# Moving low parts and half of a norm's sums to GpSimd, taking the norm's roots by columns, and placing loads and casts elsewhere in a two-layer hybrid backbone

## The chip, the core and the metric

The kernel runs on one core of a Trainium2 chip. A core has a matrix engine (TensorE, PE in the profile, with its weight loads as PEld), a vector engine (VectorE, DVE), a scalar engine (ScalarE, ACT), a general engine (GpSimd, POOL), a queue for transfers (SyncE, SP) and 16 DMA engines. Each engine works through its instructions in a fixed order and waits on semaphores. The metric is the device time of one execution in microseconds.

## The reference

`x` (1024 tokens, width 1024) goes through two layers and a final RMS norm. In the words of the reference:

```python
# layer 0 (even): conv branch A and bidirectional RG-LRU branch B
va, vg, ga, xb, gb = split(h @ w_in)
u = depthwise_conv(va * sigmoid(vg), conv_w, conv_b)
y_a = silu(layernorm(u)) * silu(ga)
y_b = rglru(xb) * silu(gb)
x = x + gate * (concat([y_a, y_b]) @ w_out)
# layer 1 (odd): pooling mixer
u, g = split(modulate(rmsnorm(x)) @ w_in)
x = x + gate * ((pool_and_group_matmul(u) * scale * silu(g)) @ w_out)
return rmsnorm(x) * final_g
```

`shift`, `scale` and `gate` of a layer come from a product of `silu(c)` with that layer's modulation matrix. All is float32. The layer norm over the width is `(u - mean) * rsqrt(var + eps)`, with `eps` 1e-5.

## The kernel before

Activations lie with the width on the 128 partitions (8 blocks, `u0` to `u7`) and the tokens along the row, in two halves of 512. A float32 product is made of three products of a shorter type: each operand is split into a high part (a cast, by ScalarE) and a low part (source less high part, by VectorE or GpSimd); TensorE adds high x high, high x low and low x high. Names ending in `h` and `l`, or beginning with `wh` and `wl`, are these parts. For the ga, woa, v, g and wo products a two by two block scheme ("quad": accumulators `qa`, `qb`, `qc`, seven products with operands `b11`, `t1`, ... `t4`) replaces the eight products.

The stages of the program in time: folds of weights (to 83 us), the input products and the LRU (to 510), the ga quads (to 587), `wob` (the half of `w_out` that meets branch B: 8 output blocks of two token halves with 24 matmuls each, 587 to 694), `woa` (the half that meets branch A, four quads, 694 to 780), more weight folds and the second layer's norm (to 828), v and g quads, the output product `wo` in two parts, and the final norm.

Up to the end of `wob` the order on each engine is the order in which the code calls `on()` (line 476 is its issuing line, so nearly all rows of that part read L476): `vec`, `act`, `gp`, `cast` and `sp` append to VectorE, ScalarE, GpSimd, casts of ScalarE and SyncE's queue. From `woa` on (`fixed[0] = False`) a scheduler orders the instructions by their readiness and priorities.

What the prediction touches, in the order before. `block_split` makes the low parts of the ga operands (8 of 128x1024) and `gated_split` those of branch B (`ybl0` to `ybl7`), all on VectorE. `wob_split(m)` casts the weights of output block m and makes their low part `wl_wob` on GpSimd. `ln_mean` multiplies the running sum `lnsum` by ones (`mu`), after three of the eight steps of block 0. `ln_square` subtracts `mu` and squares; `ln_add` sums the eight squares on VectorE, into `lnsum` again. `ln_root` multiplies this by ones (`ms_ln`, 512 wide), takes the root on ScalarE (`sq_ln`, 512 wide); `ln_scale` begins with a reciprocal of 512 columns on VectorE and multiplies the eight blocks. `ln_silus`, `ga_mult`: silu, and the product with silu(ga); `wob_evict` adds a block of `wob`, times the gate, to `xp` (ScalarE and GpSimd up to block 4, VectorE after). The second layer's modulation is a row sum of a 128x512 half of the matrix times `cH` (silu of half of `c`): `mod_half` makes 32 of them, one accumulator column each, 12 in the `wob` stage and 20 between the `woa` quads, with small sums `m` and `a` behind each. `rstd_cols` takes the second layer's root already by columns: four one-column matmuls, a root and reciprocal of 128x4, a diagonal (`dg`, identity times the four columns) and a matmul with ones. `split_x` makes the operands of the v product, `fo` the evictions of folds, and `y_operand` loads, casts and subtracts the operands of `wo` (`yr_b`, `y_b11h`); `b_wo` is a copy of an accumulator by ScalarE.

Of the kernel before, what the change touches and what calls it, by code (L numbers as in the profile page):

```python
# [54 lines left out]
def body(ctx, tc, xT, ctxT, cc, ccol, modT, modW, win, gw, wout, wu, grp, wg, wo1, small, edge, ident, outT):  # L55
# [1114 lines left out]
    def gated_split(n):  # L1170
# [3 lines left out]
        vec(nc.vector.tensor_tensor, out=bl[n], in0=raw, in1=bh[n].bitcast(F32), op=sub)  # L1174
# [121 lines left out]
    def half_c(q):  # L1296
        sp(cH, cc[0, HALF[q]].partition_broadcast(P))
        act(cH, cH, AF.Silu)

# [52 lines left out]

    def ln_scale(h):
        vec(nc.vector.reciprocal, out=lnr[h], in_=lnrt[h])
# [18 lines left out]
    mraws = []  # L1373

    def mod_load(q, n):
        mraws.append(ttile(f"mod1_{n}_{q}"))
        (sp if staged[0] else nc.sync.dma_start)(mraws[-1], modT[1, n, :, HALF[q]])

    def mod_half(q, n):
        raw = mraws.pop(0)  # L1380
        vec(nc.vector.scalar_tensor_tensor, out=raw, in0=raw, scalar=1.0, in1=cH, op0=mult, op1=mult,
            accum_out=m1p[:, n, q : q + 1])

    def mod_halves():
        for n in range(NFIX, 2 * KT):
            mod_load(0, n)
            mod_half(0, n)
            yield
        load_c(0, cH, HALF[1])
        for n in range(2 * KT):  # L1390
            mod_load(1, n)
            mod_half(1, n)
# [701 lines left out]
```

## Time and profile before

| | |
|---|---|
| median of 3 runs | 1328.02 us (1327.42 to 1328.87) |
| profiled execution | 1327.48 us, span 1325.7 us |
| granted TensorE clock, mean | 0.984 |
| busy: PE, DVE, ACT, POOL | 1275.4, 1170.1, 650.8, 393.8 us |
| instructions | 15823 |

The span runs from the first to the last instruction, and the profiled execution's own time is 1.8 us longer. A row of the waits names who waited, for whom, the sum, the count and the longest. A row of the timeline has start, duration, engine, line, operation, tiles written and read, shapes and how many instructions it joins; in brackets the idle time before it and what ended it. Durations of matmuls overlap, since they are pipelined: their pace is read from their starts.

### The profile page before, as it was taken

What the parts mean: (1) busy time and instruction counts of PE and PEld (TensorE: products, weight loads), DVE (VectorE), ACT (ScalarE), POOL (GpSimd) and SP (SyncE); (2) the same over time, 40 slices, a digit from 0 to 9 for tenths busy, and PEclk for the clock granted to TensorE, in tenths of its full rate; (3) what the DMA queues carried; (4) which work ended last, traced back from release to release, by engine and by line L of the source; (5) the groups of instructions that cost most, each with busy time, mean ns of one, the idle gap of its engine ahead of it and who ended that gap; (6) DMA issues with size and microseconds to landing.
All of it is one profiled execution on the core that took longest, in us unless ns stands there. A gap on an engine that the chain in (4) does not pass through costs nothing.

```text
span 1325.7 us, 15823 instructions
## 1 busy us (share of the span) xinstructions
PE 1275.4 (96%) x5552; PEld 1019.6 (77%) x5552; DVE 1170.1 (88%) x1790; ACT 650.8 (49%) x949; POOL 393.8 (30%) x214
## 2 busy tenths in 40 slices
PE   8999999999999999989899989899999999989996
PEld 3468888888888888867687878688878888768784
DVE  7959999999999999998988877998999987877875
ACT  5343666566566633555724345734333334634542
POOL 3063765577656626763410022000000000000002
PEclk9999999999999999999999999899999999999997
DMA  9963111112111284474556476244333334868613
GB/s 360 385 210 142 57 42 62 52 61 72 40 64 41 80 297 175 140 291 165 185 200 225 161 251 191 72 151 151 112 105 126 111 120 134 309 206 274 236 64 127
DMA packets 92083, 206.96 MB, mean 156 GB/s; under 512 B 8803, under 2 KB 28643, under 8 KB 92005
## 3 DMA queue, kind: packets, MB, share of 16 engines
q1 hardware_dynamic: 80100, 193.38, 42.3%
q10 hardware_dynamic: 11904, 12.59, 2.8%
q8 instruction: 43, 0.70, 0.2%
q14 instruction: 36, 0.29, 0.1%
HBM read 149.31 MB, written 56.62 MB: 155 GB/s over the span
## 4 chain that ended last, share of the span: by engine, by line
PE 70%; DVE 13%; DMA 10%; ACT 3%; issue 2%; POOL 1%; SPq 1%; ACTq 0%; POOLq 0%; DVEq 0%
PE gb L476 7%; PE vg L476 7%; PE va L476 7%; PE xb L476 6%; PE fold L282 4%; PE g L476 4%; PE qb_ga L476 2%; PE wob L476 2%; PE qc_ga L476 2%; PE qa_ga L476 2%; PE xbc L476 2%; DMA mod<-modT 1%; DMA wr_wu<-wu 1%; PE qb_v L989 1%; PE qb_v L991 1%
## 5 line engine op out<-in xcount | busy, mean ns | idle before, releaser
L476 DVE SCALAR_TENSOR_TENSOR conv<-u,sm,conv 128x505 f32<-128x505 f32 (+7 forms) x229 | 156.1, 746 | 0.9
L1914 POOL TENSOR_TENSOR o<-x,rr 128x256 f32<-128x256 f32 (+1 forms) x9 | 8.0, 926 | 455.0 <-ACT rr L1902 452.0
L476 POOL TENSOR_TENSOR l<-l,l 128x1280 f32<-128x1280 f32 (+1 forms) x23 | 63.9, 2794 | 83.3 <-DVE l L476 68.2
L476 ACT ACTIVATE l<-g,sm 128x512 f32<-128x512 f32 (+1 forms) x96 | 58.6, 618 | 57.8 <-PE g L476 57.0
L282 PE MATMUL fold<-graw,wu 128*128 128x512 f32 x128 | 58.5, 619 | 1.4 <-DMA wu<-wu 1.4
L104 POOL TENSOR_TENSOR wl_wu<-wr_wu,wh_wu 128x1024 fp32r<-128x1024 f32 x8 | 19.2, 2416 | 121.0 <-DVE gl L104 101.8
L476 PE MATMUL wob<-ybh,wl_wob 128*128 128x512 f32 x128 | 50.9, 397 | 4.4 <-POOL wl_wob L476 4.4
L476 PE MATMUL wob<-ybh,wh_wob 128*128 128x512 f32 x128 | 52.4, 409 | 0.7 <-ACT wh_wob L476 0.7
L282 PEld LDWEIGHTS fold<-graw,wu 128*128 128x128 f32 x128 | 25.2, 199 | 34.1 <-issue 30.3
L476 DVE SCALAR_TENSOR_TENSOR conv<-cL,wsum,conv 128x505 f32<-128x505 f32 (+7 forms) x75 | 51.2, 745 | 0.2
L103 ACT CAST wq_v<-wr_v 128x512 fp32r<-128x512 f32 x48 | 28.2, 620 | 45.6 <-DMA wr_v<-wfold 14.8
L476 PE MATMUL wob<-ybl,wh_wob 128*128 128x512 f32 x128 | 50.6, 395 | 0.0
L476 PE MATMUL gb<-h0l,wh_gb 128*128 128x512 f32 x128 | 49.8, 389 | 0.0
L476 PE MATMUL gb<-h0h,wh_gb 128*128 128x512 f32 x128 | 49.8, 389 | 0.0
L476 PE MATMUL vg<-h0l,wh_vg 128*128 128x512 f32 x128 | 49.8, 389 | 0.0
L476 PE MATMUL vg<-h0h,wl_vg 128*128 128x512 f32 x128 | 49.8, 389 | 0.0
L476 PE MATMUL vg<-h0h,wh_vg 128*128 128x512 f32 x128 | 49.8, 389 | 0.0
L476 PE MATMUL va<-h0h,wh_va 128*128 128x512 f32 x128 | 49.8, 389 | 0.0
L476 PE MATMUL va<-h0l,wh_va 128*128 128x512 f32 x128 | 49.8, 389 | 0.0
L476 PE MATMUL va<-h0h,wl_va 128*128 128x512 f32 x128 | 49.8, 389 | 0.0
L476 PE MATMUL gb<-h0h,wl_gb 128*128 128x512 f32 x128 | 49.8, 389 | 0.0
L476 DVE TENSOR_TENSOR_SCAN l<-l,l 128x256 f32<-128x256 f32 (+1 forms) x32 | 48.7, 1522 | 1.1
(695 smaller groups left out, 4376.4 us busy)
## 6 DMA issues: line engine op xcount, KB each, us to landing
mod<-modT SPq DMA_DIRECT2D x20, 512.0 KB, 8.0
x_part<-xp SPq DMA_DIRECT2D x32, 256.0 KB, 3.7
mod<-modT SPq DMA_DIRECT2D x32, 256.0 KB, 5.0
wr_v<-wfold SPq DMA_DIRECT2D x16, 512.0 KB, 4.2
wr_g<-wg SPq DMA_DIRECT2D x16, 512.0 KB, 4.9
wr_wo<-wo SPq DMA_DIRECT2D x16, 512.0 KB, 3.8
y_b<-y SPq DMA_DIRECT2D x24, 256.0 KB, 3.6
y_t<-y SPq DMA_DIRECT2D x24, 256.0 KB, 2.8
```

The lines of the kernel that those rows point to most:

```text
L103: return (nc.scalar.copy(hi, src), eng.tensor_tensor(out=lo, in0=src, in1=hi.bitcast(F32), op=sub))
L104: eng.tensor_tensor(out=lo, in0=src, in1=hi.bitcast(F32), op=sub))
L282: nc.tensor.matmul(ps, w[:, kc], gs[i], start=(i == 0), stop=(i == 3))
L476: last[eng] = f(*args, **kw)
L989: nc.tensor.matmul(ps, hi, xh[k], start=(first and k == 0), stop=False, skip_group_check=not first)
L991: nc.tensor.matmul(ps, hi, xl[k], start=False, stop=False, skip_group_check=not first)
L1914: nc.gpsimd.tensor_tensor(out=o[:, k - k0], in0=v, in1=rr, op=mult)
```

## The change

Seven edits. (1) Four of the eight ga low parts (`htl`, r = 1) and `ybl0` to `ybl3` go from VectorE to GpSimd; `wl_wob0` and `wl_wob5` to `wl_wob7` go from GpSimd to VectorE, and the casts of `wob_split` stand before the evictions of their block. (2) The two `mu` matmuls stand after seven of eight steps of block 0. (3) Of a half's squares, those of blocks 2 to 5 are added up on GpSimd into that of block 1, the last two and the join on VectorE. (4) The layer norm's roots are taken by columns, with an identity loaded into the spare end of `lnsum0`. (5) Of the second layer's modulation halves 16 are summed in the `wob` stage and 16 in the first of the `woa` stage, loaded in fours or pairs, and `m`, `a` are made by four wide operations at the end. (6) The second layer's identity is loaded early into the spare end of `n1acc0`; the stores of `x1` are issued one eviction later; the casts of `b11` and `b21` of v have priority. (7) Three operands of the second part of `wo` are loaded where they were loaded and cast before, and cast later.

The norm's place, on GpSimd, at the begin of `wob`. Before (`xp` are the residual blocks, `wo` the evicted ones):

```order
L476 TENSOR_TENSOR wl_wob1_4722<-wr_wob1_4674,wh_wob1_4721 128x1024
L476 TENSOR_TENSOR xp0_0_4701<-xp0_0_4701,wo_0_0_4851 128x512
L476 TENSOR_TENSOR xp0_1_4703<-xp0_1_4703,wo_0_1_4856 128x512
L476 TENSOR_TENSOR wl_wob2_4863<-wr_wob2_4725,wh_wob2_4862 128x1024
L476 TENSOR_TENSOR xp1_0_4854<-xp1_0_4854,wo_1_0_4920 128x512
L476 TENSOR_TENSOR xp1_1_4859<-xp1_1_4859,wo_1_1_4959 128x512
L476 TENSOR_TENSOR wl_wob3_4970<-wr_wob3_4866,wh_wob3_4969 128x1024
```

and now:

```order
L476 TENSOR_TENSOR ybl3_4588<-ybl3_4588,ybh3_4668 128x1024
L476 TENSOR_TENSOR wl_wob1_4724<-wr_wob1_4675,wh_wob1_4723 128x1024
L476 TENSOR_TENSOR lsq1_0_4812<-lsq1_0_4812,lsq2_0_4815 128x512
L476 TENSOR_TENSOR lsq1_0_4812<-lsq1_0_4812,lsq3_0_4818 128x512
L476 TENSOR_TENSOR lsq1_0_4812<-lsq1_0_4812,lsq4_0_4822 128x512
L476 TENSOR_TENSOR lsq1_0_4812<-lsq1_0_4812,lsq5_0_4826 128x512
L476 TENSOR_TENSOR xp0_0_4702<-xp0_0_4702,wo_0_0_4860 128x512
L476 TENSOR_TENSOR xp0_1_4704<-xp0_1_4704,wo_0_1_4865 128x512
L476 TENSOR_TENSOR wl_wob2_4872<-wr_wob2_4727,wh_wob2_4871 128x1024
L476 TENSOR_TENSOR lsq1_1_4855<-lsq1_1_4855,lsq2_1_4858 128x512
```

The additions of squares (`lsq`) have come between the weights' low parts. On ScalarE, where the two roots were taken (`sq_ln`), before:

```order
L476 ACTIVATE wo_1_0_4920<-wob1_0_4894,m0_176 128x512
L476 ACT_TABLE_LOAD
L476 ACTIVATE sq_ln0_4929<-ms_ln0_0_4926,eps_l_139 128x512
L476 ACTIVATE wo_1_1_4959<-wob1_1_4895,m0_176 128x512
L476 CAST wh_wob3_4969<-wr_wob3_4866 128x1024
L476 ACTIVATE wo_2_0_5001<-wob2_0_4975,m0_176 128x512
L476 ACTIVATE sq_ln1_5009<-ms_ln1_5007,eps_l_139 128x512
L476 ACTIVATE wo_2_1_5044<-wob2_1_4976,m0_176 128x512
```

and now the end of the eight silus of half 0 with the root of half 1 (`rc_ln1`):

```order
L476 ACTIVATE u3_1879<-u3_1879,sm_131 128x512
L476 ACTIVATE u7_3237<-u7_3237,sm_131 128x512
L476 ACT_TABLE_LOAD
L476 ACTIVATE rc_ln1_5048<-ms_ln1_5021,eps_l_139 128x4
L476 CAST wh_wob4_5084<-wr_wob4_4973 128x1024
L476 ACTIVATE wo_2_1_5090<-wob2_1_4995,m0_176 128x512
```

The root of half 1 stood before the silus of half 0 and now stands behind them. TensorE's matmul with the diagonal of half 1 stands between the two halves' last products of block 2 and block 3. On VectorE, the end of `woa`, before:

```order
L1535 SCALAR_TENSOR_TENSOR x1_7_6078<-qb_woa6_6081,m0_176,x1_7_6078 128x512
L1525 TENSOR_TENSOR n1acc0_5580<-n1acc0_5580,n1q6_1_0_6190 128x512
L535 SCALAR_TENSOR_TENSOR mod1_11_1_6193,m1p_3670<-mod1_11_1_6193,cH_3671 128x512
L535 SCALAR_TENSOR_TENSOR mod1_12_1_6198,m1p_3670<-mod1_12_1_6198,cH_3671 128x512
L535 SCALAR_TENSOR_TENSOR m1_178<-m1p_3670,sm_131 128x1
L535 SCALAR_TENSOR_TENSOR mod1_13_1_6203,m1p_3670<-mod1_13_1_6203,cH_3671 128x512
```

and now:

```order
L1562 SCALAR_TENSOR_TENSOR x1_7_6084<-qb_woa6_6087,m0_176,x1_7_6084 128x512
L104 TENSOR_TENSOR gl_3_0_6272<-graw_3_0_6269,gh_3_0_6271 128x1024
L1552 TENSOR_TENSOR n1acc0_5603<-n1acc0_5603,n1q6_1_0_6196 128x512
L104 TENSOR_TENSOR gl_3_1_6278<-graw_3_1_6275,gh_3_1_6277 128x1024
L203 RECIPROCAL rc_n10_6212<-rc_n10_6212 128x4
L205 TENSOR_TENSOR dg_n10_6219<-n1acc0_5603,rc_n10_6212 128x512
```

The halves (`mod1`) and small sums are no longer between the last eviction and the diagonal `dg_n10`.

The diff, cut to its core:

```diff
@@ before: line 1070
         htl.append([d2tile(f"htl{i}_{r}", F32R) for r in range(2)])
-        for r in range(2):
-            vec(nc.vector.tensor_tensor, out=htl[i][r], in0=hraw[i][r], in1=hth[i][r].bitcast(F32), op=sub)
+        for r, by in enumerate((vadd, gp)):
+            by(out=htl[i][r], in0=hraw[i][r], in1=hth[i][r].bitcast(F32), op=sub)
@@ before: line 1171
         cast(bh[n], raw)
-        vec(nc.vector.tensor_tensor, out=bl[n], in0=raw, in1=bh[n].bitcast(F32), op=sub)
+        (gp if n < KH else vadd)(out=bl[n], in0=raw, in1=bh[n].bitcast(F32), op=sub)
@@ before: line 1261
-    def wob_split(m):
+    def wob_split(m, by=None):
         if m < KT:
-            gws[KT + m] = raw_split(obs.pop(m), f"wob{m}")
+            gws[KT + m] = raw_split(obs.pop(m), f"wob{m}", by)
@@ before: line 1277
         fill(3 if n < 4 else 1)
+        if n == 2:
+            sp(idln, ident)
         if n == 3:
-            wob_split(0)
+            wob_split(0, vadd)
         if n == 4:
                 xp_load(0, h)
+            sp(cH, cc[0, HALF[0]].partition_broadcast(P))
         if n == 5:
@@ before: line 1293
-    def half_c(q):
-        sp(cH, cc[0, HALF[q]].partition_broadcast(P))
-        act(cH, cH, AF.Silu)
-
+    idln = lnacc[0][:, H : H + P]
     lnmu, lnsq = {}, {}
@@ before: line 1338
     def ln_add(j, h):
-        if j > 0:
-            vec(nc.vector.tensor_tensor, out=lnacc[h][:, :H] if j == KT - 1 else lnsq[h],
-                in0=lnsq[h], in1=lsq.pop((j, h)), op=add)
-
-    lnrt, lnr = {}, {}
+        if 1 < j < 6:
+            gp(out=lsq[1, h], in0=lsq[1, h], in1=lsq.pop((j, h)), op=add)
+        elif j > 5:
+            vadd(out=lnsq[h], in0=lnsq[h], in1=lsq.pop((j, h)), op=add)
+        if j == KT - 1:
+            vadd(out=lnacc[h][:, :H], in0=lnsq[h], in1=lsq.pop((1, h)), op=add)
+    def ln_squares(h, js):
+        for j in js:
+            ln_square(j, h)
+            if j > 1:
+                ln_add(j - 1, h)
+        if j == KT - 1:
+            ln_add(j, h)
+    lnsum, lnrt, lnr = {}, {}, {}
+    def ln_cols(h):
+        lnsum[h], lnr[h] = banks(f"ms_ln{h}", h)
+        for c in range(H // P):
+            on("pe", nc.tensor.matmul, lnsum[h][:, c : c + 1], lnacc[h][:, c * P : (c + 1) * P], ones[:, 0:1],
+               start=True, stop=True)
+    def ln_diag(h):
+        r = hpool.tile([P, H // P], F32, tag="rc", name=f"rc_ln{h}")
+        act(r, lnsum[h][:, : H // P], AF.Sqrt, bias=eps_l)
+        vec(nc.vector.reciprocal, out=r, in_=r)
+        lnrt[h] = ttile(f"dg_ln{h}")
+        vec(nc.vector.tensor_tensor, out=lnrt[h].rearrange("p (c t) -> p c t", t=P),
+            in0=idln.unsqueeze(1).to_broadcast([P, H // P, P]),
+            in1=r.unsqueeze(2).to_broadcast([P, H // P, P]), op=mult)
     def ln_root(h):
-        ps, lnr[h] = banks(f"ms_ln{h}", h)
-        on("pe", nc.tensor.matmul, ps, ones, lnacc[h][:, :H], start=True, stop=True)
-        lnrt[h] = ttile(f"sq_ln{h}")
-        act(lnrt[h], ps, AF.Sqrt, bias=eps_l)
+        on("pe", nc.tensor.matmul, lnr[h], ones, lnrt[h], start=True, stop=True)
     def ln_scale(h):
-        vec(nc.vector.reciprocal, out=lnr[h], in_=lnrt[h])
         for j in range(KT):
@@ before: line 1370
-    mraws = []
-
...
+    mraws, halved = [], [0, 0]
+    def mod_load(*raws):
+        for raw in raws:
+            q, n = divmod(halved[0], 2 * KT)
+            (sp if staged[0] else nc.sync.dma_start)(raw, modT[1, n, :, HALF[q]])
+            mraws.append(raw)
+            halved[0] += 1
     def mod_halves():
...
+        for raw in mraws:
+            q, n = divmod(halved[1], 2 * KT)
+            vec(nc.vector.scalar_tensor_tensor, out=raw, in0=raw, scalar=1.0, in1=cH, op0=mult, op1=mult,
+                accum_out=m1p[:, n, q : q + 1])
+            halved[1] += 1
+        mraws.clear()
+    def mod_pairs():
+        n = halved[0]
+        for t in [d2tile(f"mod1_{n}_{i}") for i in range(2)]:
+            mod_load(*[t[:, h] for h in HALF])
+    def mod_four(alloc):
+        mod_load(*[alloc(f"mod1_{halved[0]}_{i}") for i in range(4)])
@@ before: line 1422
                     next(steps[h])
-                if k == 2:
-                    for h in range(2):
-                        ln_mean(h)
+            for h in range(2):
+                ln_mean(h)
         for h in range(2):
             if m == 0:
...
+                if h == 0:
+                    act(cH, cH, AF.Silu)
+                    ln_squares(0, range(KT))
+                    mod_pairs()
+                else:
+                    ln_squares(1, range(3))
+                    for q in range(2):
+                        wob_evict(0, q)
+                    wob_split(2)
+                    wob_load(3)
+                    ln_squares(1, range(3, KT))
+            elif h == 0:
+                if m == 2:
+                    ln_root(0)
+                    ln_cols(1)
+                wob_evict(m, 0)
+                if m == 2:
+                    ln_scale(0)
+                    for part in range(2):
+                        ln_silus(0, part)
+                    ln_diag(1)
+                    mod_pairs()
+                elif m == 3:
+                    ln_silus(1, 0)
+                    mod_halves()
+                    for i in range(KH):
+                        ga_mult(i, 0)
+                        ga_mult(KH + i, 0)
+                elif m == 4:
+                    w0 = wquad_load([wout[q, 0] for q in range(2)], "woa0")
+                elif m > 5:
+                    mod_halves()
+                if 4 < m < 7:
+                    mod_four(ttile)
             else:
-                wob_evict(m, h)
+                if m == 1:
+                    ln_cols(0)
+                elif m == 2:
+                    ln_root(1)
+                if m < 4:
+                    wob_split(m + 2, vadd if m == 3 else None)
+                    wob_load(m + 3)
+                wob_evict(m, 1)
+                if m == 1:
+                    ln_diag(0)
+                    mod_halves()
+                elif m == 2:
+                    ln_scale(1)
+                elif m == 3:
+                    ln_silus(1, 1)
+                    for i in range(KH):
+                        ga_mult(i, 1)
+                        ga_mult(KH + i, 1)
+                if m > 3:
+                    wob_split(m + 2, vadd)
+                    wob_load(m + 3)
             if m < 2:
                     ga_load(4 * m + 2 * h + q)
-            if m >= 4:
-                mod_steps(2)
-            if (m, h) == (4, 0):
-                w0 = wquad_load([wout[q, 0] for q in range(2)], "woa0")
-        if m > 0:
-            wob_split(m + 2)
-            wob_load(m + 3)
-    mod_steps(0)
+    sp(cH, cc[0, HALF[1]].partition_broadcast(P))
+    act(cH, cH, AF.Silu)
     xouts.pop()()
@@ before: line 1515
     nacc = [atile("n1acc0"), atile("n1acc1")]
+    idn = nacc[0][:, H : H + P]
+    nc.sync.dma_start(idn, ident)
...
     fold2 = fold(2, wr_tile, vtile, d2tile, [None, None, dtile, dtile])
     for m in range(0, KT, 2):
+        mod_four(vtile)
         w0 = woa(m, w0, (lambda: wo_weights(m + 2)) if m < KT - 2 else None)
...
+        mod_halves()
+    mm1 = m1[:, 0, : 2 * KT]
+    nc.vector.tensor_tensor(out=mm1, in0=m1p[:, :, 0], in1=m1p[:, :, 1], op=add)
+    nc.vector.tensor_tensor(out=mm1, in0=mm1, in1=col(O_MB + 3 * KT, 2 * KT), op=add)
+    nc.vector.scalar_tensor_tensor(out=a1[:, 0], in0=m1[:, 0, KT : 2 * KT], scalar=1.0, in1=col(O_NG + KT, KT),
+                                   op0=add, op1=mult)
     idD = cH[:, :P]
     nc.vector.tensor_tensor(out=dsh, in0=m1[:, 0, KH:KT], in1=m1[:, 0, 0:KH], op=sub)
-    rs = [rstd_cols(nacc[h][:, :H], f"n1{h}", idD, hpool, h) for h in range(2)]
+    rs = [rstd_cols(nacc[h][:, :H], f"n1{h}", idn, hpool, h) for h in range(2)]
     for f in (fold2, fold2, fold3, fold3):
@@ before: line 1576
         else:
-            nc.scalar.activation(hi[i], src, AF.Identity, bias=shift)
+            with ExitStack() as xctx:
+                if name in ("b11", "b21"):
+                    xctx.enter_context(tc.high_priority(offset=EVAC))
+                nc.scalar.activation(hi[i], src, AF.Identity, bias=shift)
             nc.vector.scalar_tensor_tensor(out=lo[i], in0=src, scalar=shift, in1=hi[i].bitcast(F32), op0=add, op1=sub)
@@ before: line 1671
+    yraws = {}
+    def y_load(part, name, raw_tile):
+        yraws[part, name] = [raw_tile(f"yr_{part}_{name}_{q}") for q in range(2)]
+        for q in range(2):
+            nc.sync.dma_start(yraws[part, name][q], y_raw[part][name][:, q * S : (q + 1) * S])
...
@@ before: line 1816
                 with tc.issue_after(stored[0].ins):
-                    return wo1_weights(0, m + 2)
+                    w = wo1_weights(0, m + 2)
+                if m == KT - 4:
+                    y_operands(1, iter([None]), BOPS[:1], lambda name, dt: xtile(name, dt))
+                return w
             w = wo1_weights(1, 0)
+            y_operands(1, iter([None] * 2), BOPS[1:3])
             y_operands(1, iter([xtile]), BOPS[3:4])
             with tc.issue_after(loaded[0].ins):
-                y_operands(1, iter([xtile] * 2), BOPS[1:3])
+                for name in BOPS[1:3]:
+                    y_load(1, name, xtile)
         w = quad(w, f"wo0_{m}", yops[0], put, nxt)
             with tc.issue_after(loaded[0].ins):
-                y_operands(1, iter([xtile]), BOPS[:1], lambda name, dt: xtile(name, dt))
+                y_load(1, BOPS[0], xtile)
     def x2_load(m):
```

More of the change, by code (lines that the diff above doesn't have):

```diff
@@ L1534, in put @@
                 nc.sync.dma_start(v, dr)
[L1535 to L1536 removed]
+            d = nc.vector.scalar_tensor_tensor(out=v, in0=x, scalar=m0[:, 0, 2 * KT + m + i : 2 * KT + m + i + 1],
+                                               in1=v, op0=mult, op1=add)
+            while stores:
+                with tc.issue_after(d.ins):
+                    nc.sync.dma_start(*stores.pop(0))
             if part != 0:
[L1538 removed]
+                stores.append((dr, v))
                 square_acc(nacc[h][:, :H], v, (m, i) == (0, h), f"n1q{m}_{i}_{h}")
         return quad(w, f"woa{m}", ya, put, ahead)
+    stores = []
     fold2 = fold(2, wr_tile, vtile, d2tile, [None, None, dtile, dtile])
@@ L1544, in body @@
     for m in range(0, KT, 2):
+        mod_four(vtile)
         w0 = woa(m, w0, (lambda: wo_weights(m + 2)) if m < KT - 2 else None)
-        for _ in range((4, 6, 5, 5)[m // 2]):
-            next(mods)
+        mod_halves()
+    nc.sync.dma_start(*stores.pop(0))
+    mm1 = m1[:, 0, : 2 * KT]
[3 more added lines that the diff above has]
+                                   op0=add, op1=mult)
     idD = cH[:, :P]
@@ L1681, in y_operand @@
             lo.append(alloc(f"y{part}_{name}l{q}", F32R))
-            if raw_tile is None:
+            if raw_tile is None and not loaded_:
                 r = lo[q].bitcast(F32)
```

68 lines of the change are left out of this document (4 added, 64 removed).

## The prediction

> **What bounds the kernel now.** First the page, for the share of each engine:
>
> ```profile
> span 1325.7 us, 15823 instructions
> PE 1275.4 (96%) x5552; PEld 1019.6 (77%) x5552; DVE 1170.1 (88%) x1790; ACT 650.8 (49%) x949; POOL 393.8 (30%) x214
> ```
>
> TensorE is the bound: outside its waits and its slow-clock stretches nothing but fewer matmuls would shorten the program, and the change removes none. So the second view is what TensorE waited for:
>
> ```profile
> PE mu L476 <- DVE lnsum L476: 5.8, 1, 5.8
> PE wob L476 <- POOL wl_wob L476: 4.4, 2, 3.6
> ...
> PE qb_wo L989 <- ACT b_wo L1793: 3.6, 2, 2.7
> ...
> PE qb_woa L989 <- DVE m L535: 3.4, 1, 3.4
> PE qc_v L991 <- DVE x_t1l L104: 2.7, 1, 2.7
> PE qc_v L989 <- ACT fo L262: 2.4, 1, 2.4
> ```
>
> These six rows are the waits the change touches: 22.3 us in all (columns: sum, count, longest). Third, whether a wait costs more than itself: TensorE's instructions around three of them.
>
> ```profile
> 591.14 0.39 PE L476 MATMUL wob<-ybh,wl_wob 128*128 128x512 f32 x1
> 597.34 3.78 PE L476 MATMUL mu<-lnsum,ones 128*128 128x512 f32 x4 [5.80 <-DVE lnsum L476]
> ...
> 602.03 0.39 PE L476 MATMUL wob<-ybh,wh_wob 128*128 128x512 f32 x1
> 602.26 0.40 PE L476 MATMUL wob<-ybl,wh_wob 128*128 128x512 f32 x1
> ...
> 660.40 0.63 PE L476 MATMUL wob<-ybh,wh_wob 128*128 128x512 f32 x1
> 660.83 0.63 PE L476 MATMUL wob<-ybl,wh_wob 128*128 128x512 f32 x1
> ...
> 693.74 0.39 PE L989 MATMUL qa_woa<-ya_b11h,wq_woa 128*128 128x512 f32 x1
> 1189.35 0.63 PE L991 MATMUL qb_wo<-y_t4l,wq_wo 128*128 128x512 f32 x1
> ```
>
> Starts lie 0.23 us apart at full pace (602.03, 602.26) and 0.43 after the wait that ended at 659.8 (660.40, 660.83), where a matmul takes 0.63 instead of 0.39. Such a row stands too behind the 2.70 us wait of `qb_wo` (1189.35). By the rows behind them both slow stretches last about 3.4 us, eight matmuls at twice the spacing, so each costs 1.7 on top. The Trainium skill ("TensorE: Matmul & The Clock Gate", The HAM clock gate) gives one idle window of about 3.4 us as what brings the half clock; the row at 1189.35 disagrees, since the clock fell after a wait of 2.70. By that page the 2.7 us wait foreseen below would cost no clock, which makes the time 0.85 shorter; I go by the row.
>
> Where the waits come from, and how GpSimd and VectorE hinder each other:
>
> ```profile
> 583.50 4.56 DVE L476 TENSOR_TENSOR ybl<-ybl,ybh 128x1024 fp32r<-128x1024 f32 x2
> 593.20 3.48 DVE L476 TENSOR_TENSOR ybl<-ybl,ybh 128x1024 fp32r<-128x1024 f32 x3
> 584.02 2.96 POOL L476 TENSOR_TENSOR wl_wob<-wr_wob,wh_wob 128x1024 fp32r<-128x1024 f32 x1 [4.62 <-PE qc_ga L476]
> 614.35 2.40 POOL L476 TENSOR_TENSOR wl_wob<-wr_wob,wh_wob 128x1024 fp32r<-128x1024 f32 x1
> 618.49 1.29 POOL L476 TENSOR_TENSOR xp<-xp,wo 128x512 f32<-128x512 f32 x1 [1.73 <-ACT wo L476]
> ```
>
> VectorE has low parts to do until 596.7, then the two sums that `mu` waits for. Three low parts alone take 3.48 (1.16 each); two beside GpSimd's 2.96 us operation take 4.56, 2.2 more: one of them stood nearly as long as the GpSimd operation ran. So work moved to GpSimd is not free for VectorE where VectorE's operation reads two tiles of SBUF. The Trainium skill says the same and speaks against this change ("SBUF — State Buffer", Who interferes with whom): the port pair is locked for a whole instruction and "the other **fully blocks**"; its result is the last rival.
>
> **The change part by part.** Sums are made against the profiled execution, 1327.48 us (span 1325.7 and 1.8 around it); the median of the runs, 1328.02, is 0.5 above it.
>
> *A, up to `mu`.* VectorE loses eight low parts of 1.16 us (four of the ga operands, `ybl` 0 to 3), 9.3 us, and gets one weight low part of 1.2 (`wl_wob0`). GpSimd does the eight in 2.40 each. From the pair above I charge VectorE 1 us for each that meets it, so most of the 8 us goes: I let the sums end as before, at 598. (All of it kept would be 590; all eight blocking for 2.40 would be 609.) The two `mu` now stand 24 matmuls later, 24 x 0.227 = 5.4, so TensorE arrives at about 597.5 and waits 1 us, with the clock up. Before, 591.14 to 602.03 is 10.9, of which four wob matmuls (0.9) and `mu` at full pace (half of 3.78, 1.9) are work: 8.1 lost. **A = -7.1** (-8 to +5).
>
> *B, the norm's roots.* This is the term against the change, since the order puts two new points where TensorE waits for a chain. Its pieces:
>
> ```profile
> 620.44 3.36 DVE L476 RECIPROCAL ms_ln<-sq_ln 128x512 f32<-128x512 f32 x1 [0.88 <-ACT sq_ln L476]
> 623.84 4.87 DVE L476 TENSOR_TENSOR u<-u,ms_ln 128x512 f32<-128x512 f32 x8
> 618.42 1.28 ACT L476 ACT_TABLE_LOAD   x1
> 633.92 5.76 ACT L476 ACTIVATE u<-u,sm 128x512 f32<-128x512 f32 x8
> 789.31 0.26 ACT L202 ACTIVATE rc_n<-ms_n,eps_r 128x4 f32<-128x4 f32 x1
> 770.28 0.68 DVE L535 SCALAR_TENSOR_TENSOR mod<-mod,cH 128x512 f32<-128x512 f32 x1
> 796.25 0.16 DVE L203 RECIPROCAL rc_n<-rc_n 128x4 f32<-128x4 f32 x1
> 796.45 0.69 DVE L205 TENSOR_TENSOR dg_n<-cH,rc_n 128x512 f32<-128x512 f32 x1
> ```
>
> Two reciprocals of 3.36 become 0.16 plus a diagonal of 0.69: VectorE saves 5.0. But before, the matmul `ms_ln` needed only the sum of squares; now the second matmul needs root, reciprocal and diagonal, and wob3 stands behind it. wob0 ends at 601 (591.14, then 31 matmuls, 7.0, `mu` 1.9 and the wait of 1), wob1 takes 48 x 0.227 = 10.9 and the columns 1, so TensorE wants `wl_wob2` at 612.9. GpSimd has two `xp` adds (1.29) before it, whose evictions ScalarE does only behind half 0's eight squares and three of half 1, about 610; the low part (2.40) ends at about 615.6: 2.7 of wait. Then come its four adds of half 1, 5.3, and VectorE's last sum, so `lnsum1` at 621.8. VectorE's order has the diagonal of half 0 behind that `lnsum1`: 622.9, TensorE, there at 621.0, waits 1.9. Then VectorE does four modulation halves (0.68 each, 2.7), blocked by an `xp` add and `wl_wob3` (1.29, 2.40): 629.3 (625.6 unblocked). Eight scalings (4.87) follow; the silu of u4, second in ScalarE's order, needs the fifth, 632.4, and seven silus at 0.72 (5.76 / 8) end at 637.5. Only then comes ScalarE's table load 1.28 and root 0.26, then 0.16 and 0.69: the diagonal of half 1 is ready at 640.0. TensorE, after 24 matmuls (5.4) and the columns, is there at 630: a wait of 10. Sum: 2.7 + 1.9 + 10, 1.7 for the clock after the last and half of that, 0.85, after the first (2.7 is at the edge), 1.0 for the column sums added to TensorE: **B = +18.1** (+8 to +30).
>
> *C, wob3 to wob7.* The waits of 4.4 for `wl_wob` and 1.7 of clock: the low parts of wob5 to 7 go to VectorE, at 1.2 each, and the casts stand ahead of silus and evictions, half a tile earlier. With TensorE 11 us later in the same stretch and VectorE relieved of no more than it gets, I count all gone: **C = -6.1** (-7 to 0). woa starts 4.8 later, at 698.6 instead of 693.74.
>
> *D, woa0 to woa2.* ScalarE's and VectorE's operands for woa0 are as late as TensorE; 16 modulation halves instead of 6 stand among woa2's weights, 10 x 0.68 = 6.8 more for VectorE, beside gaps of about its size there. SyncE's queue holds woa4's weight loads behind those halves' loads. **D = 0** (-3 to +6).
>
> *E, F, G, later waits.* Their rows:
>
> ```profile
> 775.20 0.74 DVE L1535 SCALAR_TENSOR_TENSOR x<-qb_woa,m,x 128x512 f32<-128x512 f32 x1
> 794.03 1.16 DVE L205 TENSOR_TENSOR dg_n<-cH,rc_n 128x512 f32<-128x512 f32 x1 [2.32 <-DMA cH<-ident]
> 838.37 0.80 PE L991 MATMUL qc_v<-x_t1l,wq_v 128*128 128x512 f32 x1 [2.66 <-DVE x_t1l L104]
> 1187.23 1.04 ACT L103 CAST y_b11h<-yr_b 128x1024 fp32r<-128x1024 f32 x1 [2.33 <-DMA yr_b<-y_b]
> 1188.19 0.58 ACT L1793 COPY b_wo<-qb_wo 128x512 f32<-128x512 f32 x1
> ```
>
> E: the eviction at 775.20 stood behind modulation halves of woa6, which are now done by woa4; the wait 3.4 and 1.7 of clock go, **-5.1**. F: the diagonal waited 2.32 for the identity, which is now loaded in the wob stage, and the halves before it are gone, so all sixteen scalings start 4 or more earlier; the two waits, 2.4 and 2.7, and about 7 us of slow clock on either side of the second (0.80 where 0.39 is full pace), 3.5, are 8.6; I take **-7**, as the `fo` wait is ScalarE's own and may stay (0 to -8.6). G: the copy that TensorE waited for stood behind the cast at 1187.23, which waited for its load; load and cast now have places of their own: 2.7 and 1.7, **-4.4** (0 to -4.4). Identity, stores issued later and m1 by four wide operations only feed these.
>
> Sum: -7.1 + 18.1 - 6.1 + 0 - 5.1 - 7 - 4.4 = -11.6, or 1315.9 in the profiled time and **1316 us** as a median.
>
> **The rivals.** *The chain is short*: the GpSimd operations do not hold the modulation halves, so the scalings start at 625.6, 3.7 earlier, and `wl_wob2` and the first diagonal come in time, 4.6 and its clock 0.85 more: 1307. For it: the two meet only where they overlap in time. Against it: in the rows at 583.50 they did. *The late waits stay*: ScalarE's order around `fo` and the copy is as crowded, F and G give 4 instead of 11.4: 1323. For it: `fo` was held by ScalarE itself. *Nothing is gained*: TensorE's waits move and their sum is the same, since the bound behind them, VectorE in the norm, is no lighter; 1328. *Slower, by the lock*: eight low parts (2.40) and eight adds (1.29) on GpSimd, 29.5 us, block VectorE for their whole length; it saves 9.3 and 8 x 0.6 there, so it is 15.4 behind, of which 7 are in A and B already. The other 8.4 moves the second diagonal to 648, and the ten halves ahead of woa2's weights (6.8) are then no longer in gaps: 1316 + 15.2 = 1331. It decides from a diagonal at 648 with woa2 waiting too.
>
> **How the numbers follow.** Forecast 0.46, short chain 0.21, late waits 0.17, nothing 0.06, lock 0.10. Anything within 0.2%, 2.7 us, is no change to a measurement here. Faster is 0.84, same 0.06, slower 0.10. The forecast's own range is 1310 to 1321; to hold 8 in 10 it goes down to the short chain, 1305, and up past the late waits, 1325.
>
> **What would show it.** Right: `mu` without a wait above 2; a `ms_ln` matmul of half 1 that waits 7 to 12 us for `dg_ln`, with slow clock behind; no `wl_wob` waits after wob3; woa from 696 to 701; no row for `m`; `b_wo` without a cast ahead of it. Wrong: the diagonal ready before 635 or after 648, a new wait on woa2 or woa4 weights, or `fo` and `x_t1l` still there at 5 us.

## The result and the profile after

The changed kernel takes **1340.61 us** (median of 4, 1338.89 to 1342.21) against 1328.24 beside it (4 runs): a ratio of 1.0093, 95% interval 1.0076 to 1.0111. It is slower by 12, where 12 faster was forecast. The profiled execution has a span of 1339.4 us, 13.7 above that of before, with the same matmuls in it but for a few columns. Where the 13.7 lie is read from the first matmul of each stage in TensorE's timeline:

| stretch (start before, after) | before | after | difference | forecast |
|---|---|---|---|---|
| up to ga | 510.4 | 510.0 | -0.4 | 0 |
| ga (510.4, 510.0) | 76.9 | 83.7 | **+6.8** | 0, taken as before |
| wob to its last matmul (587.3, 593.7) | 106.6 | 111.3 | +4.7 | A + B + C = +4.9 |
| end of wob to v (693.9, 705.0) | 133.9 | 145.0 | **+11.1** | D + E = -5.1 |
| v, g to wo (827.8, 850.0) | 313.2 | 305.2 | -8.0 | F = -7 |
| wo to the end (1141.0, 1155.2) | 184.7 | 184.2 | -0.5 | G = -4.4 |

The waits of TensorE in the changed kernel (sum, count, longest):

```profile
PE ms_ln L476 <- DVE dg_ln L476: 9.7, 1, 9.7
PE qa_woa L992 <- DVE wq_woa L104: 8.5, 2, 7.5
PE qa_woa L989 <- ACT wq_woa L103: 7.3, 2, 6.4
...
PE wob L476 <- POOL wl_wob L476: 2.7, 1, 2.7
PE qb_ga L476 <- ACT cp_ga L476: 2.3, 1, 2.3
PE qc_ga L476 <- DVE s_ga L476: 2.1, 1, 2.1
PE qc_wo L989 <- ACT y_b22h L103: 1.6, 1, 1.6
```

The first and the fourth are B's, foreseen at 10 and 2.7. `mu`, `m`, `fo` and `x_t1l` are gone, as foreseen. Two groups were in no term: 15.8 us in front of woa0, and 4.4 us in the ga quads. They are the two stretches that went wrong.

**In front of woa0.** One sum of GpSimd's, the residual `xp` of block 3, half 1, is the first thing that is late. GpSimd's row in the timeline, and VectorE's at its end (start, duration, engine, line, operation):

```profile
665.91 14.72 POOL L476 TENSOR_TENSOR xp<-xp,wo 128x512 f32<-128x512 f32 x1 [7.32 <-ACT wo L476]
...
679.40 0.74 DVE L1318 SCALAR_TENSOR_TENSOR xp<-wob,m,xp 128x512 f32<-128x512 f32 x1
```

What VectorE did from 665.91 to 679.40, the largest of its groups by line and form (count, then busy time, mean ns of one, idle time):

```profile
L476 DVE TENSOR_TENSOR u<-u,gat 128x512 f32<-128x512 f32 x8 | 5.1, 679 | 0.0
```

And the same stretch as a window over all engines: its length, busy time and count of PE, PEld, DVE, ACT and POOL, then clock, DMA share and GB/s:

```profile
665.91:679.40 13.49, 13.49 (x61) 11.19 (x60) 13.49 (x23) 5.93 (x9) 13.49 (x1) 1.00 0.00 0
```

Such a sum takes 1.28 to 1.74 elsewhere in this trace and 14.72 here. VectorE is busy for all of the 13.49 us; 22 operations fall in it, its products and low parts among them, at their usual pace (0.68 for 128x512), each a `TENSOR_TENSOR` with both inputs in SBUF; no byte is moved by DMA. The sum ends 1.23 after 679.40, when VectorE begins the first operation with an input in PSUM (`wob`). If that is the cause, the lock of the prediction's last rival works the other way round here: VectorE shuts GpSimd out, and not for one instruction but for a run of them. The run with four copies, below, tests this.

The delay is carried by SyncE's queue. SyncE, VectorE, ScalarE and TensorE, from their timelines:

```profile
660.90 0.33 SPq L476 DMA_DIRECT2D xp<-xT  x1
680.66 0.33 SPq L476 DMA_DIRECT2D x_part<-xp  x1
...
683.75 0.38 SPq L476 DMA_DIRECT2D wr_wob<-wout  x1
...
700.55 0.97 SPq L476 DMA_DIRECT2D mod<-modT  x2
...
704.53 0.69 DVE L476 SCALAR_TENSOR_TENSOR mod<-mod,cH 128x512 f32<-128x512 f32 x1 [6.70 <-DMA mod<-modT]
...
705.87 0.62 ACT L103 CAST ya_t2h<-yat 128x512 fp32r<-128x512 f32 x1 [14.98 <-DVE yat L1525]
...
711.47 0.79 PE L989 MATMUL qa_woa<-ya_b11h,wq_woa 128*128 128x512 f32 x1 [6.43 <-ACT wq_woa L103]
```

The store of the late sum holds the queue from 661 to 680.66, and the weights of woa0 and wob7 and the modulation halves stand behind it. The later `xp` loads wait for buffers that a store must first empty (the queue stands from 693.6 to 699.70 for one), so the last four halves of the wob stage are issued only from 700.55 on, when wob is nearly over; VectorE waits 6.70 for one, with `yat` behind it; ScalarE waits 14.98 for `yat`, with woa0's weight cast behind that (710.80 to 711.41); TensorE waits 6.43, and at 720.17 another 7.48, for a low part that VectorE makes behind the rest.

**The ga quads.** This stage as a window (columns as above), of the kernel before:

```profile
510.40:587.30 76.90, 76.49 (x338) 62.99 (x337) 73.99 (x105) 39.12 (x64) 56.35 (x40) 1.00 0.51 181
```

and of the changed one:

```profile
510.00:593.70 83.70, 78.66 (x338) 64.02 (x337) 77.36 (x111) 40.04 (x65) 62.71 (x43) 0.98 0.51 182
```

Near its end, a store that ScalarE issues (ACTq), in the timeline of before:

```profile
577.04 0.33 ACTq L476 DMA_DIRECT2D ga_raw<-s_ga  x1
```

and of the changed kernel:

```profile
580.83 0.63 ACT L476 ACTIVATE s_ga<-s_ga 128x512 f32<-128x512 f32 x1
583.56 0.33 ACTq L476 DMA_DIRECT2D ga_raw<-s_ga  x1
583.93 0.62 ACT L476 CAST wq_ga6q<-wr_ga6q 128x512 fp32r<-128x512 f32 x1 [2.46 <-DMA ybl<-yb_raw]
```

Of an early quad, VectorE's last operation on `s_ga`, before:

```profile
529.66 0.69 DVE L476 TENSOR_TENSOR s_ga<-qc_ga,s_ga 128x512 f32<-128x512 f32 x1
```

and in the changed kernel:

```profile
534.08 0.68 DVE L476 TENSOR_TENSOR s_ga<-qc_ga,s_ga 128x512 f32<-128x512 f32 x1
```

TensorE stood still for 0.4 us of this stage before, and now for 5.0 (the length of the window less TensorE's busy time). VectorE reaches `s_ga` 4.4 later, for which TensorE waits 2.1 with half clock behind; and the store, whose silu ends at 581.46, is issued at 583.56, with all of ScalarE's casts behind it. In the program its issue waits on a counter of finished transfers that it shares with SyncE's loads: before, the load it waits for is that of `ybl3`, now it is that of `ybl4`, because the norm's identity, loaded among them, moved every later load one place on.

### The profile page after: what moved, and what is told of

The parts are those of the page before. It is cut to its first block, busy times and chain, and to the rows that moved or that the text cites. A ratio compares the mean times of both kernels' runs of the same rounds, so it can differ in the third digit from the quotient of the medians.

```text
span 1339.4 us, 15854 instructions
## 1 busy us (share of the span) xinstructions
PE 1278.1 (95%) x5568; PEld 1023.4 (76%) x5568; DVE 1158.6 (87%) x1759; ACT 652.4 (49%) x951; POOL 426.6 (32%) x226
## 4 chain that ended last, share of the span: by engine, by line
PE 61%; DVE 18%; DMA 9%; issue 4%; POOL 4%; ACT 3%; SPq 1%; POOLq 0%; ACTq 0%; DVEq 0%
PE vg L476 7%; PE va L476 6%; PE xb L476 6%; PE fold L282 4%; PE g L476 4%; DMA x_part<-xp 2%; PE gb L476 2%; PE xbc L476 2%; DVE hraw L476 1%; DMA mod<-modT 1%; POOL xp L476 1%; PE fold L257 1%; PE fold L258 1%; PE fold L259 1%; DVE yr L476 1%
```

## The experiments

Ratios are each to the kernel before on the same chip, with 95% intervals; "us" of a difference is the difference of ratios times 1328.

**The ga low parts back on VectorE.**

```diff
-        for r, by in enumerate((vadd, gp)):
+        for r, by in enumerate((vadd, vadd)):
```


> The changed kernel with edit 1 undone in part: all eight low parts of the ga operands are VectorE's again; all else as changed. Theory L (the lock, first part): GpSimd's four low parts delay VectorE before the ga quads, so that the sums s_ga come 3 to 4 us late, TensorE waits 2.1 + 0.6 + 2.35 there and loses 1.7 of clock. By L these waits go, wob starts 5 to 7 us earlier (587 to 589 instead of 593.7) and the time falls from 1340.6 to 1334 to 1336. Rival: VectorE needs the relief, eight low parts of its own make it as late as the lock does: no change, 1339 to 1342.

1339.56 us, 1.0077 (1.0056 to 1.0098): 2 us less than the change, no more than the intervals' width. A miss. The wait for `s_ga` fell to 0.6, but wob starts at 593.3 (593.7), since that for `cp_ga` grew. From the waits:

```profile
PE qb_ga L476 <- ACT cp_ga L476: 3.9, 1, 3.9
```

and from ScalarE's timeline:

```profile
581.13 0.62 ACT L476 CAST wq_ga6q<-wr_ga6q 128x512 fp32r<-128x512 f32 x1 [3.97 <-DMA ybl<-yb_raw]
```

ScalarE reaches the store 4.3 earlier (577.15), and stands there 3.6 instead of 2.1. So the stage is no shorter (83.7): what the low parts gave back, the store took. The wait for `s_ga` is 2.1 in each of the six traces with the four low parts on GpSimd, and 1.7 or less in the six with them on VectorE.

**The identity's load out of the ga operands,** on top of that edit.

```diff
-        if n == 2:
-            sp(idln, ident)
...
                     wob_load(3)
+                    sp(idln, ident)
                     ln_squares(1, range(3, KT))
```


> The run with the low parts back on VectorE (1339.6, wob from 593.3) and one load moved: the layer norm's identity is loaded behind the last ga stores instead of among their operands. Theory S (ScalarE's store of half 0 of ga4 waits until an earlier SyncE load has landed, and the identity made that the load of ybl4, issued at 573 to 578, where it was ybl3's before): the store of ga_raw4 leaves as in the kernel before, the 3.9 us wait of qb_ga for cp_ga is below 1, wob starts at 588 to 590, and the time is about 1335. Rival (ScalarE is late for another reason, the order of its casts): cp_ga still waits 3 or more, wob starts at 593, 1339.

1337.45 us, 1.0057 (1.0038 to 1.0075). The store goes out at 579.04, 0.3 after its silu, the wait for `cp_ga` falls to 0.6, and wob starts at 589.2 instead of 593.3. ScalarE's timeline:

```profile
579.41 0.62 ACT L476 CAST wq_ga6q<-wr_ga6q 128x512 fp32r<-128x512 f32 x1 [0.64 <-DMA ybl<-yb_raw]
```

Theory S holds for the stage, 4.1 us by the place of one load of 64 KB that nobody there uses; the time fell by 2.7, with an interval as wide. The wait for `s_ga` was 1.7 here, where the run before had 0.6 with the same program up to there. The load moved with the low parts left on GpSimd was not run.

**The sums of blocks 3 and 4 away from GpSimd.** VectorE takes them from PSUM in one operation, as it does for blocks 5 to 7 already.

```diff
-        if m > 4:
+        if m > 2:
             nc.vector.scalar_tensor_tensor(out=t, in0=wob_ps[m][h], scalar=gate, in1=t, op0=mult, op1=add)
```


> The changed kernel with the residual adds of blocks 3 and 4 of wob taken from ScalarE and GpSimd and done by VectorE out of the accumulator, as blocks 5 to 7 are. Theory L (the lock, second part): the add of block 3's second half stood on GpSimd for 14.7 us because VectorE ran 20 operations with two SBUF inputs without a gap; its store held SyncE's queue for 19 us, and wob7's weights and the modulation halves, loaded by that queue, came late, so TensorE waited 6.4 + 7.5 at woa0 with the clock at half. By L SyncE has no such hold, the waits at woa0 fall under 4 together, and the time falls to 1325 to 1330. Rival Q: the modulation halves ahead of VectorE's operands wait for their own buffers, and GpSimd's late add is a bystander: the waits stay, 1338 to 1343.

1334.99 us, 1.0050 (1.0030 to 1.0069), 5.7 less than the change. The store leaves at 666.86 instead of 680.66, and the waits in front of woa0 fall from 15.8 to about 3.

v starts 11.4 earlier (838.6), of which v to the end gives 5 back, with new waits (4.1 us of `qb_v` for `vp`): probably because the scheduler ordered this part otherwise, which was not tested; so the waits came as theory L had them and the time did not (1325 to 1330). The edit also takes work from ScalarE, so it does not show the lock by itself.

**Four copies of one column.** GpSimd keeps its sums; VectorE reads one column of PSUM between the products.

```diff
                         ga_mult(KH + i, 1)
+                        pk = hpool.tile([P, 1], F32, tag="pk", name=f"pk{i}")
+                        vec(nc.vector.tensor_copy, out=pk, in_=wob_ps[3][1][:, 0:1])
```


> The changed kernel, with four copies of one column from PSUM put between VectorE's products of half 1 of block 3, and nothing else. GpSimd keeps its sums of blocks 3 and 4. Theory L2 (GpSimd's sum at 665.9 took 14.7 us because VectorE ran operations with two SBUF inputs back to back, and ended when VectorE did one with an input in PSUM): with the copies the sum is done in 2 to 4 us, its store leaves SyncE by 670 to 672 instead of 680.7, the woa0 waits (8.5 and 7.3) fall to 5 in all or less, and the time is 1325 to 1333. Rival (the sum was long for another reason, such as the DMA traffic, or any two-input operation on VectorE slows it in proportion): the sum still takes 10 us or more and the time is the change's, 1339.

1331.73 us, 1.0024 (1.0006 to 1.0041): **9.2 less than the change, by adding four operations of 0.14 us.** GpSimd's sum and VectorE beside it, in the timeline:

```profile
666.81 3.73 POOL L476 TENSOR_TENSOR xp<-xp,wo 128x512 f32<-128x512 f32 x1 [7.54 <-ACT wo L476]
669.30 0.14 DVE L476 COPY pk<-wob 128x1 f32<-128x1 f32 x1
669.37 2.32 DVE L476 TENSOR_TENSOR u<-u,gat 128x512 f32<-128x512 f32 x2
```

The sum ends at 670.54, 1.24 after the first copy began (1.23 after 679.40 in the change), and two products that take 1.28 then take 2.32: now VectorE stands. The store leaves at 670.56, the waits for `wq_woa` are 3.4 in all, and wob's end to v takes 132.7 instead of 145.0, 1.2 under the kernel before. The rival, that any two-input operation slows the sum in proportion, falls with it. With the copies the stretch from wob's end to v is 12.3 shorter than in the change, and nothing else was altered.

**Fewer modulation halves in wob.** Eight of sixteen leave the second half of `wob` and stand among the quads.

```diff
-                elif m > 5:
-                    mod_halves()
-                if 4 < m < 7:
-                    mod_four(ttile)
...
         mod_halves()
+        if m < 4:
+            mod_four(vtile)
+            mod_halves()
...
```


> The changed kernel without the 8 modulation halves in the second half of wob; 24 stand among woa0 to woa6 instead of 16. Theory L2 (the starved sum and SyncE's queue): the sum at about 666 still takes 14 us, for no half stands in that run of VectorE, and its store and the load of wr_wob7 behind it are as late; only the 6.7 us in which VectorE waited for the halves' loads goes, so about half of the woa0 waits stays: 1332 to 1336. Rival Q (the halves and their loads alone hold woa0): the woa0 waits go, woa starts within 1 us of the end of wob, 1325 or less.

1338.03 us, 1.0065 (1.0051 to 1.0079). Neither theory had it whole. The sum is starved as before, until VectorE runs out of work at 681.23 (680.56 + 0.67), in the timeline:

```profile
666.18 16.22 POOL L476 TENSOR_TENSOR xp<-xp,wo 128x512 f32<-128x512 f32 x1 [7.63 <-ACT wo L476]
680.56 0.67 DVE L1519 TENSOR_TENSOR yat<-u,u 128x512 f32<-128x512 f32 x1
```

and from the waits:

```profile
PE wob L476 <- DVE wl_wob L476: 5.7, 1, 5.7
```

The waits at woa0 are gone, as rival Q said, but the late load of wob7's weights now shows in front of wob7 (5.7), and wob takes 119.8 instead of 111.3. The halves carried the delay to woa0; they did not make it.

**The second diagonal ahead of the silus.**

```diff
                     ln_scale(0)
+                    ln_diag(1)
                     for part in range(2):
                         ln_silus(0, part)
-                    ln_diag(1)
```


> The changed kernel with ScalarE's root and the diagonal of half 1 ahead of the silus of half 0. Term B of the prediction: TensorE's wait for dg_ln1 was 9.7, of which eight silus, a table load and the root are 9. They go behind, so the wait falls to 0 to 3 and wob3 starts 7 to 10 us earlier (639 to 641 instead of 648.5); if all of it reaches the end, 1331 to 1334. Rival: the bound behind it is VectorE's chain of scalings, products and operands, which starts at the same time: wob ends earlier, woa waits longer, 1338 to 1342.

1337.71 us, 1.0058 (1.0037 to 1.0079), 4.6 less than the change. The diagonal no longer waits for ScalarE's silus and table; its wait falls from 9.7 to 5.2, not to the 0 to 3 expected, and it comes right behind the scalings, at 640.70. What VectorE does ahead of them, in its timeline:

```profile
628.95 2.83 DVE L476 SCALAR_TENSOR_TENSOR mod<-mod,cH 128x512 f32<-128x512 f32 x1
...
635.72 4.86 DVE L476 TENSOR_TENSOR u<-u,ms_ln 128x512 f32<-128x512 f32 x8
```

The waits in front of woa0 are as in the change (7.1 and 10.0): the diagonal's lateness is no cause of them. What is left of B should then be ahead of the scalings: four modulation halves that take 6.8 us beside GpSimd. A later run moves them.

**Three edits together** (the low parts back on VectorE, the sums of blocks 3 and 4 off GpSimd, the second diagonal ahead), and **with the identity's load moved.**

> The three edits together. If the three losses lie one after the other on the path (theory L with term B): 1340.6 less 6, 13 and 7, 1311 to 1319, faster than the kernel before. If they hide each other, that is if two of them are the same VectorE time seen at two places: 1322 to 1330.

> The three edits together (1326.7, wob from 592.0, 2.9 us of wait for cp_ga) and the identity's load moved. Theory S: the cp_ga wait goes, wob starts at 588 to 589, and everything behind it is earlier by 3 to 4: 1323. Rival (ScalarE's lateness is taken up later by the diagonal's wait, which does not hang on where wob starts): 1326.

1326.68 us, 0.9976 (0.9962 to 0.9990), then 1322.16 us, 0.9939 (0.9915 to 0.9964). The three are worth 2.1, 5.7 and 4.6 alone, 12.4, and 15.5 together, which their intervals allow as a plain sum. The time lies where the losses were expected to hide each other, but by these figures they don't: each was smaller than the 6, 13 and 7 put down for it. The load is worth 4.9 more; wob starts at 587.2 instead of 592.0, and before the change it was 587.3. So the low parts and the load, undone together, account for the ga stage's loss. Their shares are known to some 2 us only: the program of the run at 1337.45 is the same up to wob, and its ga stage took 79.0 where this one took 76.9.

**The first modulation halves behind the scalings,** on top of these four.

```diff
                     ln_diag(0)
-                    mod_halves()
...
                         ln_silus(0, part)
+                    mod_halves()
                     mod_pairs()
```


> As e_idnthree, and the first four modulation halves stand on VectorE behind the scalings of half 0 and the second diagonal instead of ahead of them. Theory L (GpSimd's operations stretched these four from 2.7 to 6.8 us, and the eight scalings and the diagonal stood behind them): scalings from about 624 to 629, diagonal by 630, the 5 us wait for dg_ln and its half clock gone: 1316 to 1318. Rival (the lock only moves, the scalings run beside the same GpSimd operations and take as much longer): the wait stays at 3 to 5, 1322.

**1314.74 us, 0.9882 (0.9860 to 0.9905)**: faster than both kernels, 7.6 under the run without this edit. VectorE's timeline at the two roots:

```profile
624.49 4.87 DVE L476 TENSOR_TENSOR u<-u,ms_ln 128x512 f32<-128x512 f32 x8 [1.40 <-PE ms_ln L476]
...
629.48 0.69 DVE L476 TENSOR_TENSOR dg_ln<-lnsum,rc_ln 128x512 f32<-128x512 f32 x1
630.09 0.68 DVE L476 SCALAR_TENSOR_TENSOR mod<-mod,cH 128x512 f32<-128x512 f32 x1
```

The scalings run at full pace beside the GpSimd operations that stretched the halves (one of their inputs, `ms_ln`, is in PSUM), the halves behind them take 0.68 again, and no wait for `dg_ln` is left.

**wob2's low part on VectorE,** to take away B's 2.7.

```diff
-                    wob_split(2)
+                    wob_split(2, vadd)
```


> As the best so far (1314.7), and the low part of wob2's weights is made by VectorE, which waits there for GpSimd's sums of squares, instead of by GpSimd behind two xp sums. Term B's first wait (2.7 us of TensorE for wl_wob2 and its half clock) goes and GpSimd's four sums of half 1 start 2.4 earlier: 1310 to 1312. Rival (VectorE's operations there take the time back from the scalings, or the low part waits for its cast, which stands behind an eviction): 1314.

1320.39 us, 0.9929 (0.9916 to 0.9942): 6 slower than without it. The rival held in its mechanism, though it named 1314; in VectorE's timeline:

```profile
615.00 2.13 DVE L476 TENSOR_TENSOR wl_wob<-wr_wob,wh_wob 128x1024 fp32r<-128x1024 f32 x1 [2.84 <-ACT wh_wob L476]
```

VectorE stands 2.84 for the cast, takes 2.13 instead of 1.2 beside GpSimd, and five of half 1's subtractions, which the norm's second sum needs, stand behind. A wait for `dg_ln` of 2.7 is back. About half of the loss lies elsewhere: its ga stage took 80.0 instead of 76.7, though the program is the same up to there, as one execution differs from the next (below).

**Edit 7 undone.**

```diff
...
-            y_operands(1, iter([None] * 2), BOPS[1:3])
...
-                for name in BOPS[1:3]:
-                    y_load(1, name, xtile)
+                y_operands(1, iter([xtile] * 2), BOPS[1:3])
...
```


> The changed kernel with its edit 7 undone: three operands of the second part of wo are cast where they are loaded, as before. If term G was right as forecast, the copy b_wo waits again behind the cast of y_b11 and the time is 4.4 longer than the change, 1345. If the edit gives its gain back in the waits at 1255 (qc_wo for y_b22h 1.6, qb_wo for b_wo 0.9, and the half clock there), those are gone, b_wo's wait of 2.7 and its half clock are back at about 1200, and the time is 1339 to 1342, the same.

1343.80 us, 1.0091 (1.0064 to 1.0118), the same as the change. The profiled execution is 4.3 longer in span and 5.1 longer from wo to the end of the matmuls, with the wait back (2.7 before, 0.9 in the change):

```profile
PE qb_wo L989 <- ACT b_wo L1843: 4.7, 2, 3.8
```

By its place in the trace the edit does what G said; the timed ratio, good to 3.6 us either way, does not show it. The wait for `y_b22h` is there too (2.3, against 1.6 in the change and 0.2 before), so edit 7 does not make it.

## Why the prediction was wrong

*A* was right behind its own starting point, and that point was wrong. There was no `mu` wait, as foreseen. But "I let the sums end as before, at 598" took the start of wob as given: the sums ended at 604.7, 6.7 later, and 6.4 of that is wob's later start. It priced the eight low parts by when the sums end, not by who waits on the way. In the stage where four of them stand, TensorE stood for 0.4 before and for 5.0 now, with slow clock: +6.8, a term that the sum does not have. Of this the low parts are a part, and the identity's load, which the prediction did not cost at all ("identity ... only feed these"), is 4.1 to 4.8.

*B* was right in size and in mechanism: 9.7 for the second diagonal (10 foreseen), 2.7 for `wl_wob2`, four halves that take 6.8 us (6.4 counted), the silus and the table load ahead of the root. The first diagonal's 1.9 did not come. The diagonal came at 647.3 instead of 640.0, 6.4 of it by the later start of wob. Its two parts are removed one by one in the runs at 1337.71 and 1314.74.

*C* was right: no `wl_wob` wait after wob2. The stretch of A, B and C as a whole is +4.7 (+4.9).

*D* is the step that failed most: "0 (-3 to +6)", and it measured about +16 (11.1, and the 5.1 of E, if E came whole). Its first sentence, that the operands for woa0 are "as late as TensorE", is what failed: ScalarE's weight cast and VectorE's low part came 6.4 and 7.5 after TensorE wanted them. At woa2 and woa4, where it looked for trouble, little came: behind 720.17 no wait up to v is above 1.04. It named the modulation halves and SyncE's queue, and held the halves against gaps of VectorE. It did not ask what VectorE's ceaseless work does to the GpSimd sum whose store heads that queue. By the run with the copies that one sum is 12.3 of it; the rest is open. The rows at 583.50 and 584.02 were read in one direction only, GpSimd hinders VectorE. The Trainium skill ("SBUF — State Buffer", Who interferes with whom) has the other one as well, since by it whoever starts first has the port and the other waits until the first finishes; but by that rule the sum would have waited for the rest of one instruction, 1.21 at most, and the trace differs: it waited through 22 in 13.49 us.

*E and F* were right: no row for `m`, none for `fo` and `x_t1l`, and -8.0 in F's stretch where -7 was taken. *G* was right on its wait, but the stretch gained 0.5 where 4.4 was taken. The wait of 1.6 for `y_b22h` and the half clock behind it are 3 to 4 us of the difference; why that wait came is open, since it is also there without edit 7.

Of the signs named for being wrong none came clearly: the diagonal, at 647.3, was within its bounds by 0.7. Of those for being right one failed, the start of woa: 711.5 instead of 696 to 701. Of the rivals "slower, by the lock" had the sign and 1331, and the wrong victim: its mark, a diagonal at 648 with woa2 waiting, came as 647.3 with woa0 waiting, and neither for its reason. The sum of what was foreseen, -11.6, and the two stretches that were not, 6.8 and 16, is +11, and 13.7 was measured; most of the rest is what G did not bring.

## What to carry to other kernels

Where work moves to GpSimd, ask both ways: whom it blocks, and whether VectorE has a long stretch of operations with two inputs in SBUF that may keep it out; here one operation on PSUM in between let it in. Then ask what stands behind GpSimd's result in an in-order queue: here one store held loads of weights for 19 us. And a load added among others can cost more than itself even when it is small: here it changed which load a store waited for, so look at who waits on the loads around it.

## What the runs showed that was not expected

**How GpSimd gets in.** In the change, the run with the copies and the run with fewer halves the starved sum ended 1.17 to 1.24 us after VectorE began something else than a two-SBUF-input operation or stopped: a 0.74 operation on PSUM, a 0.14 copy from PSUM, nothing. The window in the run with fewer halves is as full as that in the change, 24 operations in 15.05 us.

In all six traces that leave this sum on GpSimd without the copies it was kept out so, for 14.3 to 16.6 us. But two such operations in a row do not always keep GpSimd out. The sum of the other half of block 3, in the changed kernel, and the next sum in the run with the copies:

```profile
656.95 1.64 POOL L476 TENSOR_TENSOR xp<-xp,wo 128x512 f32<-128x512 f32 x1 [6.01 <-ACT wo L476]
```
```profile
671.25 1.58 POOL L476 TENSOR_TENSOR xp<-xp,wo 128x512 f32<-128x512 f32 x1 [0.71 <-ACT wo L476]
```

Both came while VectorE ran operations with two inputs in SBUF, and both ended 1.2 after the next boundary between two of these (657.36 and 671.61); the VectorE operation behind the second took 1.77 instead of 0.68. What decides between the two outcomes is open. Whether an operation of VectorE with one input in SBUF would let GpSimd in as the copies did was not tried either.

**The clock falls after a wait of 2.1, or does not.** TensorE's rows behind the wait for `s_ga`, in the change and in the run with the four copies, which is the same program up to there:

```profile
534.91 0.47 PE L476 MATMUL qc_ga<-hth,wq_ga2q 128*128 128x512 f32 x1 [2.10 <-DVE s_ga L476]
...
536.06 0.63 PE L476 MATMUL qc_ga<-htl,wq_ga2q 128*128 128x512 f32 x1
```
```profile
535.06 0.47 PE L476 MATMUL qc_ga<-hth,wq_ga2q 128*128 128x512 f32 x1 [2.08 <-DVE s_ga L476]
...
536.05 0.39 PE L476 MATMUL qc_ga<-htl,wq_ga2q 128*128 128x512 f32 x1
```

2.10 brought 3.4 us of half clock, 1.7 on top, and 2.08 none. So in these two traces a price for the clock on a wait near 2 us is a chance, not a sum; the prediction had put the edge at 2.7. The Trainium skill ("TensorE: Matmul & The Clock Gate", The HAM clock gate) gives one idle window of about 3.4 us for it; the rows here put the edge lower.
